# Three seven-product pairs per gate-up group, ring places for split weights and stored sums in an fp32 encoder layer

## The chip, the cores and the metric

The kernel runs on one core of a Trainium2 chip. The metric is device time in microseconds (us), the median of several executions. TensorE is called PE here (PEld is its weight load), VectorE DVE, ScalarE ACT, GpSimd POOL, and SP is the engine that issues most DMAs.

## What is computed

One encoder layer on x of 256 tokens by 2048 features, in fp32, weights drawn once per call from memory:

```
x = x + 0.5 * post1(swiglu_1(pre1(x)))
h = pre_m(x); p = h @ W_in
x = x + post_m(concat(hgrn2(p), attention(p)) @ W_out)
x = x + 0.5 * post2(swiglu_2(pre2(x)))

def swiglu(x, w_gate_up, w_down):
    gate, up = jnp.split(x @ w_gate_up, 2, axis=-1)
    return (jax.nn.silu(gate) * up) @ w_down
```

`w_gate_up` is 2048 x 11264 and `w_down` 5632 x 2048, so the two FFNs hold most of the work, and the change lies in them and in the helper that all stages use to split weights.

## The kernel before, in words

**Splits.** Every fp32 operand of a product is kept as two parts: an upper part h (ACT rounds it, L176) and a lower part l = value - h (DVE subtracts, L177; both lines are `split_act`). One block product is three matmuls into one PSUM bank, `three` (L417, issued at L423): upper by upper, upper by lower, lower by upper. Weights come by `load` (L141) as a `raw` tile of 128 x 2048 words, of which three places exist (`rawp`, L68). `split` (L158) cuts it by two calls of `split_half` (L168), 1024 columns each, into h and l places of 1024 columns; the pools `hip` and `lop` have five places each (L69, L70).

**Gate-up stage.** `Gated` (L793) does 11 groups of 512 gate and 512 up columns in each FFN. A group is eight pairs (u = 0 to 7), each pair a slice of 256 of the 2048 rows and so one raw tile of four blocks b11, b12, b21, b22 of 128 x 512. A plain pair (`plain`, L432) is eight block products, 24 matmuls. A pair that stands in `gated.sums` goes through `seven` (L445): seven products in place of eight (21 matmuls), of sums of weight blocks with sums of activation blocks. On the weight side `seven` splits b11 into a place of its own (`one_block`, L438, here a place of `hip` and `lop` of which half is used), adds on DVE at L455 (1024 columns), splits the lower half, adds at L459, splits the upper half, adds at L461 and splits the lower half again (`last`). Four extra banks p collect products that belong to several results; `fold` (L489) adds them to the four result banks c once per group, by one ACT copy (L495) and eight DVE adds (L496 to L503), issued just ahead of the products of the pair at position `after` + 1, where `after` is the position behind the last seven-product pair (L406). The two pairs around the fold have their products sorted by result bank. Which pairs are seven-product pairs is `MIXED_IN = (2, 4)` (L787). Their activation sums are made once per FFN by `even` (L860), during group 0; `begin` (L398) looks them up when a group begins, so group 0 of each FFN is all plain.

**Units.** Behind each group `units` (L881) makes silu(gate) * up (L886 ACT, L887 DVE), turns it by eight 128 x 128 transposes (L898) into two tiles `ht`, splits these, and for 11 of the 22 tiles (`MIXED`, L788) also makes four sums of 128 x 128 (`sums_of`, L378: L380, L383, L384). These are kept in fp32, in the room where X was and in other pools (`sums_room`, L850).

**Down stage.** `Pairs` (L540) multiplies the 22 tiles by `w_down` in two runs of 1024 result columns, 11 plain and 11 seven-product pairs in a run, in the order written out at L934. In each seven-product pair `left_sums` (L569) splits the fp32 sums of that tile into the tile `sp` again, in both runs, but for two tiles whose split is kept from run 0 to run 1 (`keep`). Here `seven` also loads and half splits the next plain pair from inside (`begin_next`, L505). The same class does the output projection of the middle stage (sums `sy`).

**Order.** The order of instructions on each engine is set when the kernel is built, from program order and the builder's own estimates of time; only the start (L959) and the end of each down stage (`finish`, L631) are issued as written. Every engine and DMA queue then works in its order.

Of the kernel before, what the change touches and what calls it, by code (L numbers as in the profile page):

```python
# [20 lines left out]
P = 128  # L21
# [16 lines left out]
def hymba_layer_kernel(  # L38
# [27 lines left out]
    const = ctx.enter_context(tc.tile_pool(name="const", bufs=1))  # L66
    xp = ctx.enter_context(tc.tile_pool(name="xp", bufs=1))
    rawp = ctx.enter_context(tc.tile_pool(name="rawp", bufs=3))  # L68
    hip = ctx.enter_context(tc.tile_pool(name="hip", bufs=5))  # L69
    lop = ctx.enter_context(tc.tile_pool(name="lop", bufs=5))  # L70
    psum = ctx.enter_context(tc.tile_pool(name="psum", bufs=4, space=bass.MemoryType.PSUM))
    dram = ctx.enter_context(tc.tile_pool(name="dram", bufs=1, space=bass.MemoryType.DRAM))

# [64 lines left out]
    scales = const.tile([P, 8], F32, tag="scales", name="scales")  # L138
    rs2, two, rest = (scales[:, 2 * i : 2 * i + 2] for i in range(3))

    def load(src, between=None):  # L141
        raw = rawp.tile([P, 2048], F32, tag="raw", name=nm("raw"))
        if len(src.shape) == 4:

            dst = raw.rearrange("p (a n b) -> p a n b", a=src.shape[1], n=src.shape[2])
            parts = [(dst[:, a], src[:, a]) for a in range(src.shape[1])]
        else:
            parts = [(raw.rearrange("p (a b) -> p a b", a=src.shape[1]), src)]
        for i, (to, of) in enumerate(parts):
            if i and between:  # L150
                between()
            nc.sync.dma_start(to, of)
        return raw

    def split_load(src, hp=hip, lp=lop, between=None, middle=None):
        return split(load(src, between), hp, lp, middle)

    def split(raw, hp=hip, lp=lop, middle=None):  # L158
        hs, ls = [], []
        for i in range(2):  # L160
            if i and middle:
                middle()
            h, l = split_half(raw, i, hp, lp)
            hs.append(h)
            ls.append(l)
        return hs, ls

    def split_half(raw, i, hp=hip, lp=lop):  # L168
        part = raw[:, i * 1024 : (i + 1) * 1024]
        h = hp.tile([P, 1024], F32R, tag="h", name=nm("h"))  # L170
        l = lp.tile([P, 1024], F32R, tag="l", name=nm("l"))
        split_act(h, l, part)
        return h, l

# [212 lines left out]
    class Blocks:  # L387
# [50 lines left out]
        def one_block(self):  # L438

            return (  # L440
                p.tile([P, 1024], F32R, tag=t, name=nm(t))[:, 0:512]
                for p, t in ((hip, "h"), (lop, "l"))
            )

        def seven(self, u, aside=None):  # L445

            raw = load(self.source(u))
            if aside:
                aside()
            b11, b12, b21, b22 = (raw[:, i * 512 : (i + 1) * 512] for i in range(4))  # L450
            four = raw.rearrange("p (i c) -> p i c", i=4)
            h, l = self.one_block()
            split_act(h, l, b11)

            nc.vector.tensor_tensor(  # L455
                four[:, 0:2], four[:, 0::3], four[:, 1:2].to_broadcast([P, 2, 512]), ALU.add
            )
            lower = split_half(raw, 1)
            nc.vector.tensor_tensor(b22, b11, b22, ALU.add)  # L459
            upper = split_half(raw, 0)  # L460
            nc.vector.tensor_tensor(b21, b22, b21, ALU.add)  # L461
            if aside:
                aside()
            last = split_half(raw, 1)
            if not self.p:
                self.p = [pa(), pa(), pb(), pb()]
            a, w = self.tiles[u], self.left_sums(u)

            def lhs(k, m):
                return [a[:, k, i, m * P : (m + 1) * P] for i in range(2)]  # L470

            def summed(j):
                return [w[:, j, i, :] for i in range(2)]

            def rhs(two, n):
                return [x[:, n * 512 : (n + 1) * 512] for x in two]

            for at, left, right in (
                (("p", 0), lhs(0, 0), (h, l)),
                (("c", 0, 0), lhs(1, 0), rhs(lower, 0)),  # L480
                (("c", 0, 1), summed(S4), rhs(lower, 1)),
                (("p", 1), summed(S1), rhs(upper, 0)),
                (("p", 3), summed(S3), rhs(upper, 1)),
                (("p", 2), summed(S2), rhs(last, 1)),
                (("c", 1, 0), lhs(1, 1), rhs(last, 0)),
            ):
                self.three(at, *left, *right)

        def fold(self):  # L489

# [49 lines left out]
    class Pairs(Blocks):  # L540
# [4 lines left out]
        HELD = 2  # L545
        AHEAD = True

        def __init__(self, w, orders, tiles, sums, room, gain_src, keep=()):

            super().__init__(tiles, sums)  # L550
            self.keep, self.kept = keep, {}
# [15 lines left out]
            return src.rearrange("(k p) c -> p k c", p=P)  # L567

        def left_sums(self, u):  # L569
            if u in self.kept:  # L570
                return self.kept[u]
            keep = self.now == 0 and u in self.keep
            tag = f"sp{u}" if keep else "sp"
            w = far["pool"].tile([P, 4, 2, P], F32R, tag=tag, name=nm("sp"), bufs=1 if keep else 2)
            split_act(w[:, :, 0, :], w[:, :, 1, :], self.sums[u])
            if keep:
                self.kept[u] = w
            return w

        def one_block(self):  # L580
            return (
# [49 lines left out]
        def finish(self, mul, post, new_x=None, gain=None, lead=None):  # L631
# [5 lines left out]
            self.work(n_order - self.HELD)  # L637
            held = []
            for u in order[n_order - self.HELD :]:
                held.append((u, *split_load(self.source(u), hp=post, lp=post)))  # L640
            close_far()
            self.half_gain(post)
            if new_x:
# [140 lines left out]
    NU = DFF // 256  # L784
    LATE = 8

    MIXED_IN = (2, 4)  # L787
    MIXED = (*range(0, 18, 2), 20, 21)  # L788

    def pair_of(xt, u):  # L790
# [2 lines left out]
    class Gated(Blocks):  # L793
# [13 lines left out]

        def left_sums(self, u):
            return self.sums[u]

        def see(self, xt):
            for u in range(KT // 2):
# [24 lines left out]
    def ffn(gated, w_dn, post_gain, again, gain=None, lead=None, aside=None):  # L837

        with ExitStack() as st:
# [5 lines left out]
            where_X_was = []  # L845

            def room_for(tag):
                return work.tile([P, 512], F32, tag=tag, name=nm(tag))

            def sums_room(u):  # L850
                n = MIXED.index(u)
                if n == 0:
                    where_X_was.append(xp.tile([P, 8, 4, P], F32, tag="X", name=nm("sums")))
                if n < 8:
                    return where_X_was[0][:, n]
                if n > 8:
                    return far["pool"].tile([P, 4, P], F32, tag=f"su{n}", name=nm("su"), bufs=1)
                return work.tile([P, 4, P], F32, tag=f"su{n}", name=nm("su"))

            def even(u):  # L860

                x = gated.tiles[u].rearrange("p k i t -> p (k i) t")
                nc.vector.tensor_tensor(
                    x, x.bitcast(F32), R[:, None, :].to_broadcast([P, 4, T]), ALU.mult
                )
                if u in MIXED_IN:
                    x = gated.tiles[u].bitcast(F32)
                    whole = room_for("z").rearrange("p (k t) -> p k t", k=2)
                    nc.vector.tensor_tensor(whole, x[:, :, 0, :], x[:, :, 1, :], ALU.add)
                    ws = sums_of(whole, room_for("s").rearrange("p (j t) -> p j t", j=4))  # L870
                    w = work.tile([P, 4, 2, P], F32R, tag="sp", name=nm("xs"), bufs=2)
                    split_act(w[:, :, 0, :], w[:, :, 1, :], ws)
                    gated.sums[u] = w

# [6 lines left out]
            def units(c, scale):  # L881
# [10 lines left out]
                for j in range(2):  # L892
# [15 lines left out]
                    split_act(ht[:, :, 0, :], ht[:, :, 1, :], u)  # L908
                    hts.append(ht)
                    if g in MIXED:  # L910
                        sums[g] = sums_of(u, sums_room(g))
                yield

            pre_stats()
# [1 line left out]
            for g in range(NG):  # L916
                if g:
                    gated.group(g)
                for u in range(gated.pos, KT // 2):
                    gated.work(u + 1)  # L920
                    if g == 0:
                        if u == 4:
                            power_and_rest()
                            spread(two)
                        for done in {4: (0, 1, 2), 5: (3, 4), 6: (5, 6), 7: (7,)}.get(u, ()):
                            even(done)
                        if u == 5 and aside:
                            aside()
                    if waiting and u == 0:
                        next(waiting)  # L930
                waiting = units(gated.c, rest if g else rs2)
                next(waiting)
            close_far()
            orders = [  # L934
                [1, 0, 3, 2, 4, 5, 6, 8, 7, 10, 9, 12, 11, 14, 13, 16, 15, 20, 21, 17, 18, 19],

                [1, 0, 2, 3, 4, 5, 6, 14, 7, 8, 9, 10, 16, 11, 12, 13, 20, 21, 15, 17, 18, 19],
            ]
            sums.update((u, None) for u in MIXED if u not in sums)
            rows = Pairs(w_dn, orders, hts, sums, work, post_gain, keep=(0, 2))  # L940
            rows.half_gain(far["pool"])
            rows.work(1)
            next(waiting)
# [15 lines left out]
    with tc.manual_schedule():  # L959
# [15 lines left out]
        h, l = (  # L975
            p.tile([P, 1024], F32R, tag=t, name=nm(t)) for p, t in ((hip, "h"), (lop, "l"))
        )

        def half(i):
            cs = slice(i * 512, (i + 1) * 512)  # L980
# [549 lines left out]
```

## Time and profile before

| | |
|---|---|
| median of 3 runs | 1864.88 us (1864.38 to 1866.83) |
| span of the profiled execution, first to last instruction | 1861.4 us |
| PE busy | 1840.7 us, 99% of the span |
| DVE busy | 1576.6 us, 85% |
| ACT busy | 1086.1 us, 58% |
| DMA | 365.78 MB, mean 197 GB/s |
| granted TensorE clock, mean | 0.998 of full speed (2.4 GHz level) |

The profiled execution has no time of its own beside its span; the runs' median lies 3.5 us above that span. The gate-up stages lie at about 10 to 487 us and 1150 to 1620 us, the down stages behind them to about 720 us and to the end. A matmul's record is longer than the step from one matmul to the next, since matmuls are pipelined; starts tell the pace.

### The profile page before, as it was taken

How to read it: one execution, taken by the hardware profiler on the slowest of the kernel's cores; microseconds unless marked ns; L12 is line 12 of the kernel's file. 1: busy time of each engine (PE TensorE's matmuls, PEld its weight loads, DVE VectorE, ACT ScalarE, POOL GpSimd, SP SyncE). 2: the span in 40 equal slices, each digit the busy share in tenths (PEclk: the TensorE clock that was granted, in tenths of full speed). 3: DMA queues.
4: the chain of work that ended last, by engine and by line, in shares of the span. 5: the costliest groups of instructions: out<-in, count | busy, mean ns of one | idle time of the engine just before them, and what ended most of it. 6: DMA issues, size and time to landing. Idle time of an engine off the chain costs nothing.

```text
span 1861.4 us, 23279 instructions
## 1 busy us (share of the span) xinstructions
PE 1840.7 (99%) x8658; PEld 1527.0 (82%) x8658; DVE 1576.6 (85%) x1988; ACT 1086.1 (58%) x1445; POOL 21.4 (1%) x39
## 2 busy tenths in 40 slices
PE   9999999999999999999999999999999999999997
PEld 6888888888878777888888887788888888878886
DVE  7978888888899998567787788888888788899997
ACT  6555555555566565676677655655555555566563
POOL 1000000000000000000000000000000000000000
PEclk9999999999999999999999999999999999999999
DMA  7555655555555465655565455565565556445564
GB/s 251 204 200 187 208 196 181 181 203 203 188 204 215 179 255 196 201 181 166 169 187 148 169 210 200 185 214 186 211 207 192 199 195 207 175 181 205 224 228 168
DMA packets 180880, 365.78 MB, mean 197 GB/s; under 512 B 9256, under 2 KB 56448, under 8 KB 180000
## 3 DMA queue, kind: packets, MB, share of 16 engines
q1 hardware_dynamic: 180416, 364.17, 56.2%
q8 instruction: 68, 1.11, 0.2%
q14 instruction: 44, 0.36, 0.1%
q0 software_dynamic: 352, 0.14, 0.0%
HBM read 360.06 MB, written 4.21 MB: 196 GB/s over the span
## 4 chain that ended last, share of the span: by engine, by line
PE 72%; DVE 17%; DMA 4%; ACT 3%; issue 3%; POOL 0%; SPq 0%; DVEq 0%; ACTq 0%; POOLq 0%
PE pa L423 28%; PE pb L423 26%; DVE l L177 9%; PE pa L299 8%; PE pa L304 4%; DMA raw<-in_w_ffn_down_dram 2%; DVE raw L455 2%; ACT h L176 2%; DVE raw L459 1%; DVE raw L461 1%; DVE la L177 1%; DMA raw<-in_w_ffn_gate_up_dram 1%; PE pa L354 1%; PE pa L352 1%; PE pa L353 1%
## 5 line engine op out<-in xcount | busy, mean ns | idle before, releaser
L176 ACT CAST h<-raw 128x1024 fp32r<-128x1024 f32 (+1 forms) x793 | 795.0, 1028 | 616.2 <-PE pb L423 316.7
L177 DVE TENSOR_TENSOR l<-raw,h 128x1024 fp32r<-128x1024 f32 (+1 forms) x793 | 925.9, 1192 | 202.3 <-ACT h L176 168.8
L423 PE MATMUL pa<-h,xt 128*128 128x512 f32 x1248 | 431.3, 392 | 0.0
L423 PE MATMUL pb<-h,xt 128*128 128x512 f32 x1168 | 407.3, 390 | 0.0
L423 PEld LDWEIGHTS pa<-h,xt 128*128 128x128 f32 x1248 | 234.1, 188 | 48.7 <-ACT h L176 0.8
L423 PEld LDWEIGHTS pb<-h,xt 128*128 128x128 f32 x1168 | 219.2, 188 | 46.0 <-DVE xt L232 0.5
L423 PE MATMUL pa<-l,xt 128*128 128x512 f32 x624 | 243.3, 390 | 0.1
L423 PE MATMUL pb<-l,xt 128*128 128x512 f32 x584 | 227.3, 389 | 0.0
L299 PE MATMUL pa<-xt,h 128*128 128x512 f32 x672 | 164.7, 394 | 0.0
L423 PE MATMUL pa<-h,ht 128*128 128x512 f32 x440 | 156.1, 390 | 0.4 <-ACT h L176 0.4
L423 PE MATMUL pb<-h,ht 128*128 128x512 f32 x440 | 155.0, 390 | 0.2
L299 PEld LDWEIGHTS pa<-xt,h 128*128 128x128 f32 x672 | 123.0, 188 | 23.6
L423 PEld LDWEIGHTS pa<-l,xt 128*128 128x128 f32 x624 | 117.2, 188 | 24.5 <-DVE l L177 1.1
L423 PEld LDWEIGHTS pb<-l,xt 128*128 128x128 f32 x584 | 109.7, 188 | 22.6
L455 DVE TENSOR_TENSOR raw<-raw 128x1024 f32<-128x1024 f32 x88 | 107.5, 1222 | 1.6
L423 PEld LDWEIGHTS pa<-h,ht 128*128 128x128 f32 x440 | 82.4, 188 | 18.7 <-ACT h L176 1.3
L423 PEld LDWEIGHTS pb<-h,ht 128*128 128x128 f32 x440 | 82.6, 188 | 17.9 <-DVE pb L501 1.0
L304 PE MATMUL pa<-xt,l 128*128 128x256 f32 x672 | 91.5, 285 | 0.0
L304 PEld LDWEIGHTS pa<-xt,l 128*128 128x128 f32 x672 | 87.1, 191 | 3.2
L423 PE MATMUL pa<-l,ht 128*128 128x512 f32 x220 | 86.2, 392 | 1.5 <-DVE l L177 1.5
L423 PE MATMUL pb<-l,ht 128*128 128x512 f32 x220 | 86.0, 391 | 0.1
L423 PE MATMUL pb<-h,sp 128*128 128x512 f32 x192 | 70.1, 395 | 2.3 <-ACT h L176 2.3
(281 smaller groups left out, 2179.4 us busy)
## 6 DMA issues: line engine op xcount, KB each, us to landing
raw<-in_w_ffn_gate_up_dram SPq DMA_DIRECT2D x350, 512.0 KB, 4.6
raw<-in_w_ffn_down_dram SPq DMA_DIRECT2D x88, 1024.0 KB, 5.4
raw<-in_w_mix_in_dram SPq DMA_DIRECT2D x52, 1024.0 KB, 5.0
raw<-in_w_mix_out_dram SPq DMA_DIRECT2D x16, 1024.0 KB, 5.0
pg<-in_post_norm_ffn_dram SPq DMA_DIRECT2D x4, 512.0 KB, 6.9
X<-in_x_dram SPq DMA_DIRECT2D x2, 1024.0 KB, 7.4
bias<-row SPq DMA_DIRECT2D x16, 128.0 KB, 4.6
kept<-X SPq DMA_DIRECT2D x2, 1024.0 KB, 4.9
```

Source lines behind the costliest of these rows:

```text
L176: nc.scalar.copy(hi, src)
L177: nc.vector.tensor_tensor(lo, src, hi.bitcast(F32), ALU.subtract)
L299: nc.tensor.matmul(slot[f], weights(hs, kk, f), xcol(xt, k), start=(k == 0), stop=(k == KT - 1))
L304: nc.tensor.matmul(slot[f][:, 0:T], weights(ls, kk, f), xcol(xt, kh * 8 + kk, 0), start=False, stop=False,)
L352: nc.tensor.matmul(dst, xh, h[:, o : o + n], start=(k == 0), stop=False)
L353: nc.tensor.matmul(dst, xh, l[:, o : o + n], start=False, stop=False)
L354: nc.tensor.matmul(dst, xl, h[:, o : o + n], start=False, stop=(k == KT - 1))
L423: nc.tensor.matmul(self.bank(at), lhs, rhs, start=(n == 1), stop=n in (ends, self.of[at]), skip_group_check=n > ends,)
L455: nc.vector.tensor_tensor(four[:, 0:2], four[:, 0::3], four[:, 1:2].to_broadcast([P, 2, 512]), ALU.add)
L459: nc.vector.tensor_tensor(b22, b11, b22, ALU.add)
L461: nc.vector.tensor_tensor(b21, b22, b21, ALU.add)
```

## The change

- `MIXED_IN` is (1, 3, 5): three of a gate-up group's eight pairs go by seven products, and the fold moves to the group's last pair. `one_block` of the gate-up stage no longer takes a ring place but alternates between two rooms where X was.
- The pools of h and l places become two tiles, `ring_h` and `ring_l`, of five places each, taken in turn by `places`. Where two places taken together lie side by side, one subtraction of 2048 columns makes both lower parts; where they run over the ring's end, there are two of 1024.
- `seven` splits `upper` and `last` together, behind both adds.
- The activation sums of the down stage are split once, when a unit is made, and stored to device memory by a DMA from POOL's queue (128 x 1024 words each); each seven-product pair of the down stage loads them by a DMA on SP's queue (`left_early`, four places). `keep` goes, and the order of the first run is another.

```diff
-    hip = ctx.enter_context(tc.tile_pool(name="hip", bufs=5))
-    lop = ctx.enter_context(tc.tile_pool(name="lop", bufs=5))
+    ringp = ctx.enter_context(tc.tile_pool(name="ringp", bufs=1))
...
+    RING = 5
+    ring_h, ring_l = (
+        ringp.tile([P, RING * 1024], F32R, tag=t, name=f"ring{t}") for t in "hl"
+    )
+    ring = [0]
+
+    def places(n):
+        out = []
+        while n:
+            at = ring[0] % RING
+            some = min(n, RING - at)
+            ring[0] += some
+            n -= some
+            cs = slice(at * 1024, (at + some) * 1024)
+            out.append((ring_h[:, cs], ring_l[:, cs]))
+        return out
...
+    def split(raw, pool=None):
+        if pool:
+            hs, ls = zip(*(split_half(raw, i, pool) for i in range(2)))
+            return hs, ls
         hs, ls = [], []
...
+        n = 0
+        for h, l in places(2):
+            some = h.shape[1]
+            part = raw[:, n : n + some]
+            n += some
+            for o in range(0, some, 1024):
+                nc.scalar.copy(h[:, o : o + 1024], part[:, o : o + 1024])
+                hs.append(h[:, o : o + 1024])
+                ls.append(l[:, o : o + 1024])
+            nc.vector.tensor_tensor(l, part, h.bitcast(F32), ALU.subtract)
         return hs, ls
...
         def seven(self, u, aside=None):
+            self.left_early(u)
             raw = load(self.source(u))
...
             lower = split_half(raw, 1)
             nc.vector.tensor_tensor(b22, b11, b22, ALU.add)
-            upper = split_half(raw, 0)
             nc.vector.tensor_tensor(b21, b22, b21, ALU.add)
             if aside:
                 aside()
-            last = split_half(raw, 1)
+            upper, last = zip(*split(raw))
...
         def left_sums(self, u):
-            if u in self.kept:
-                return self.kept[u]
-            keep = self.now == 0 and u in self.keep
...
+            if u in self.left:
+                return self.left.pop(u)
+            w = far["pool"].tile(
+                [P, 4, 2, P], F32R, tag="sp", name=nm("sp"), bufs=4 if self.stored else 2
+            )
+            if self.stored:
+                nc.sync.dma_start(w.bitcast(F32), self.sums[u])
+            else:
+                split_act(w[:, :, 0, :], w[:, :, 1, :], self.sums[u])
             return w
...
-    MIXED_IN = (2, 4)
+    MIXED_IN = (1, 3, 5)
...
+        def one_block(self):
+            self.blocks.reverse()
+            return self.blocks[0]
...
                     if g in MIXED:
-                        sums[g] = sums_of(u, sums_room(g))
+                        ws = sums_of(u, room_for("s").rearrange("p (j t) -> p j t", j=4))
+                        w = where_X_was(0).rearrange("p (j i t) -> p j i t", j=4, i=2)
+                        split_act(w[:, :, 0, :], w[:, :, 1, :], ws)
+                        sums[g] = dram.tile([P, 4, 2, P], F32, tag=f"ss{g}", name=nm("ss"))
+                        nc.gpsimd.dma_start(sums[g], w.bitcast(F32))
...
             orders = [
-                [1, 0, 3, 2, 4, 5, 6, 8, 7, 10, 9, 12, 11, 14, 13, 16, 15, 20, 21, 17, 18, 19],
+                [1, 3, 0, 5, 2, 4, 7, 6, 8, 9, 10, 11, 12, 13, 14, 15, 16, 20, 17, 21, 18, 19],
...
-            rows = Pairs(w_dn, orders, hts, sums, work, post_gain, keep=(0, 2))
+            rows = Pairs(w_dn, orders, hts, sums, work, post_gain, stored=True)
```

## Rows read from the trace of the kernel before

**Rows 1.** The page: busy time by engine, and the chain that ended last.
```profile
PE 1840.7 (99%) x8658; PEld 1527.0 (82%) x8658; DVE 1576.6 (85%) x1988; ACT 1086.1 (58%) x1445; POOL 21.4 (1%) x39
PE 72%; DVE 17%; DMA 4%; ACT 3%; issue 3%; POOL 0%; SPq 0%; DVEq 0%; ACTq 0%; POOLq 0%
```

**Rows 2.** Busy time of each engine in stretches; here one gate-up group's length.
```profile
core 0: us, PE busy (x) PEld busy (x) DVE busy (x) ACT busy (x) POOL busy (x), PEclk, DMA share, GB/s
273.00:316.00 43.00, 43.00 (x195) 35.72 (x194) 35.73 (x43) 22.94 (x27) 0.00 (x0) 1.00 0.56 196
```

**Rows 3.** The same view for stretches of the two down stages.
```profile
500.00:550.00 50.00, 48.93 (x209) 38.41 (x208) 49.10 (x59) 28.56 (x34) 0.00 (x0) 1.00 0.57 209
...
600.00:650.00 50.00, 49.36 (x216) 40.01 (x216) 46.94 (x52) 29.86 (x40) 0.00 (x0) 1.00 0.51 183
650.00:690.00 40.00, 40.00 (x176) 32.31 (x175) 38.77 (x44) 23.94 (x28) 0.00 (x0) 1.00 0.73 269
...
1630.00:1680.00 50.00, 49.23 (x212) 38.88 (x211) 49.96 (x62) 30.55 (x37) 0.00 (x0) 1.00 0.54 197
...
1730.00:1780.00 50.00, 50.00 (x221) 40.99 (x220) 47.82 (x52) 30.61 (x40) 0.00 (x0) 1.00 0.49 175
```

**Rows 4.** PE in order of time in one gate-up group: start us, us, what.
```profile
229.95 0.39 PE L423 MATMUL pb<-h,xt 128*128 128x512 f32 x1
...
235.39 0.39 PE L423 MATMUL pb<-h,xt 128*128 128x512 f32 x1
235.62 0.27 PE L898 MATMUL pa<-ident,z 128*128 128x128 f32 x1
...
236.41 0.48 PE L423 MATMUL pa<-h,xt 128*128 128x512 f32 x1
```

**Rows 5.** DVE in order of time: two groups' ends, both sevens of one group.
```profile
229.88 0.75 DVE L887 SCALAR_TENSOR_TENSOR z<-pa,scales,z 128x512 f32<-128x512 f32 x1
...
231.91 1.22 DVE L455 TENSOR_TENSOR raw<-raw 128x1024 f32<-128x1024 f32 x1
234.22 1.22 DVE L177 TENSOR_TENSOR l<-raw,h 128x1024 fp32r<-128x1024 f32 x1 [1.08 <-ACT h L176]
...
250.51 0.69 DVE L461 TENSOR_TENSOR raw<-raw 128x512 f32<-128x512 f32 x1
252.40 4.69 DVE L177 TENSOR_TENSOR l<-raw,h 128x1024 fp32r<-128x1024 f32 x4 [1.20 <-ACT h L176]
...
272.93 0.75 DVE L887 SCALAR_TENSOR_TENSOR z<-pa,scales,z 128x512 f32<-128x512 f32 x1
```

**Rows 6.** Groups by line and shape, whole span: count, busy us, mean ns, idle before.
```profile
L177 DVE TENSOR_TENSOR l<-raw,h 128x1024 fp32r<-128x1024 f32 x751 | 899.3, 1221 | 202.1 <-ACT h L176 168.7 <-PE pa L304 29.7
L176 ACT CAST h<-raw 128x1024 fp32r<-128x1024 f32 x751 | 769.3, 1051 | 614.9 <-PE pb L423 316.7 <-DVE raw L461 96.1 <-DVE raw L455 82.0
L177 DVE TENSOR_TENSOR sp<-sums,sp 128x512 fp32r<-128x512 f32 x28 | 19.2, 684 | 0.0
L177 DVE TENSOR_TENSOR sp<-su,sp 128x512 fp32r<-128x512 f32 x12 | 8.2, 685 | 0.0
```

**Rows 7.** Waits in two gate-up groups, 273 to 359 us: us in total, times, longest.
```profile
ACT h L176 <- PE pb L423: 30.3, 16, 3.9
DVE l L177 <- ACT h L176: 14.4, 13, 2.3
```

**Rows 8.** Waits in the first down stage, 500 to 690 us.
```profile
ACT ha L176 <- DMA raw<-in_w_ffn_down_dram: 9.2, 6, 2.3
DVE l L177 <- ACT h L176: 5.7, 9, 1.2
```

**Rows 9.** DMA issues: kind, engine, count, KB each, median us to landing.
```profile
raw<-in_w_ffn_down_dram SPq DMA_DIRECT2D x88, 1024.0 KB, 5.4
kept<-X SPq DMA_DIRECT2D x2, 1024.0 KB, 4.9
row<-bias_rows POOLq DMA_DIRECT2D x1, 16.0 KB, 1.8
```

More of the change, by code (lines that the diff above doesn't have):

```diff
@@ L153, in load, with split_load, split_half @@
         return raw
-    def split_load(src, hp=hip, lp=lop, between=None, middle=None):
-        return split(load(src, between), hp, lp, middle)
-    def split(raw, hp=hip, lp=lop, middle=None):
-        hs, ls = [], []
[L160 to L165, printed above, removed]
+    def split_load(src, pool=None, between=None):
+        return split(load(src, between), pool)
+    def split(raw, pool=None):
+        if pool:
+            hs, ls = zip(*(split_half(raw, i, pool) for i in range(2)))
+            return hs, ls
+        hs, ls = [], []
+        n = 0
[8 more added lines that the diff above has]
+            nc.vector.tensor_tensor(l, part, h.bitcast(F32), ALU.subtract)
         return hs, ls
-    def split_half(raw, i, hp=hip, lp=lop):
+    def split_half(raw, i, pool=None):
         part = raw[:, i * 1024 : (i + 1) * 1024]
-        h = hp.tile([P, 1024], F32R, tag="h", name=nm("h"))
-        l = lp.tile([P, 1024], F32R, tag="l", name=nm("l"))
+        if pool:
+            h, l = (pool.tile([P, 1024], F32R, tag=t, name=nm(t)) for t in "hl")
+        else:
+            [(h, l)] = places(1)
         split_act(h, l, part)
@@ L436, in plain @@
             self.three(("c", m, n), a[:, k, 0, ms], a[:, k, 1, ms], hs[k][:, cs], ls[k][:, cs])
[L438 to L443, printed above, removed]
         def seven(self, u, aside=None):
+            self.left_early(u)
             raw = load(self.source(u))
@@ L487, in seven, with left_early @@
                 self.three(at, *left, *right)
+        def left_early(self, u):
+            pass
         def fold(self):
@@ L546, in hymba_layer_kernel, with __init__ @@
         AHEAD = True
-        def __init__(self, w, orders, tiles, sums, room, gain_src, keep=()):
+        def __init__(self, w, orders, tiles, sums, room, gain_src, stored=False):
             super().__init__(tiles, sums)
-            self.keep, self.kept = keep, {}
+            self.stored, self.left = stored, {}
             self.w, self.orders = w, orders
@@ L569, in left_sums, with left_early @@
         def left_sums(self, u):
-            if u in self.kept:
-                return self.kept[u]
-            keep = self.now == 0 and u in self.keep
[L573 to L577, printed above, removed]
-            return w
+            if u in self.left:
[5 more added lines that the diff above has]
+                nc.sync.dma_start(w.bitcast(F32), self.sums[u])
+            else:
+                split_act(w[:, :, 0, :], w[:, :, 1, :], self.sums[u])
+            return w
+        def left_early(self, u):
+            if self.stored:
+                self.left[u] = self.left_sums(u)
         def one_block(self):
@@ L639, in finish @@
             for u in order[n_order - self.HELD :]:
-                held.append((u, *split_load(self.source(u), hp=post, lp=post)))
+                held.append((u, *split_load(self.source(u), post)))
             close_far()
@@ L844, in ffn, with where_X_was @@
             hts, sums = [], {}
-            where_X_was = []
+            rooms = []
             def room_for(tag):
                 return work.tile([P, 512], F32, tag=tag, name=nm(tag))
[L850 to L858, printed above, removed]
+            def where_X_was(i):
+                if not rooms:
+                    t = xp.tile([P, 4, 1024], F32R, tag="X", name=nm("rooms"))
+                    rooms.extend(t[:, i] for i in range(4))
+                return rooms[i]
             def even(u):
@@ L870, in even @@
                     ws = sums_of(whole, room_for("s").rearrange("p (j t) -> p j t", j=4))
-                    w = work.tile([P, 4, 2, P], F32R, tag="sp", name=nm("xs"), bufs=2)
+                    if MIXED_IN.index(u) == 2:
+                        w = where_X_was(1).rearrange("p (j i t) -> p j i t", j=4, i=2)
+                    else:
+                        w = work.tile([P, 4, 2, P], F32R, tag="sp", name=nm("xs"), bufs=2)
                     split_act(w[:, :, 0, :], w[:, :, 1, :], ws)
@@ L928, in ffn @@
                             aside()
+                        if u == 6:
+                            gated.blocks = [
+                                tuple(where_X_was(2 + i)[:, o : o + 512] for o in (0, 512))
+                                for i in range(2)
+                            ]
                     if waiting and u == 0:
@@ L973, in arrive @@
             nc.sync.dma_start(raw[:, i * 512 : (i + 1) * 512], first[:, i // 2, i % 2])
-        h, l = (
-            p.tile([P, 1024], F32R, tag=t, name=nm(t)) for p, t in ((hip, "h"), (lop, "l"))
-        )
+        [(h, l)] = places(1)
         def half(i):
```

## The prediction, made before the changed kernel ran

> **What bounds the kernel now.** I read the page first. PE is busy for 99% of the span and holds 72% of the chain that ended last, DVE 17% [rows 1]; so a matmul taken away counts, unless DVE, at 85%, has no room for what is put in its place. Both differ by stage, so the stretches come next.
>
> In the gate-up stage PE is never idle, and DVE is busy for 35.73 of 43.00 us [rows 2]. The cause of DVE's other 7 us shows in the waits: in two groups DVE stood 14.4 us until ACT's upper part came, while ACT stood 30.3 us for PE to free a place [rows 7]. The chain runs back to PE: DVE is ahead, and the five places are full. PE's order of time gives the pace: 24 steps from 229.95 to 235.39 us, 0.2267 us each, at the full granted clock; the eight transposes between units take 0.79 us [rows 4]. 186 matmuls and the transposes make 42.96 us; from one group's first L887 on DVE to the next it is 43.05 [rows 5]. Nothing is lost there.
>
> The down stage is otherwise. DVE is busy for 49.10 and 49.96 of 50 us in the first stretch of each [rows 3], and PE gets through 209, 216 and 212 matmuls where a full stretch has 221. These three lose 26 matmuls, 26 x 0.2267 = 5.9 us. There DVE is the bound, and it is filled to 98% and more in spite of the dependences inside `seven`: it stood only 5.7 us for ACT in 190 [rows 8].
>
> **The change, part by part.**
>
> Gate-up, PE. A third seven-product pair takes 24 - 21 = 3 matmuls from a group. Group 0 of each FFN has none, since the activation sums do not exist when it begins, so 2 x 10 groups change: 60 x 0.2267 = **-13.6 us**. By the record's length of 0.39 us [rows 4] it would be 23, but records overlap; starts decide. The group's bound by PE becomes 43.05 - 0.68 = 42.37 us.
>
> Gate-up, DVE. A plain pair that becomes a seven costs one 512 split, L455, L459, L461 and a third 1024 split more. Four 1024 splits back to back took 4.69 us and the last of them 1.22 alone, so a step is 1.16 [rows 5, 6]; a 512 step is by the same overlap 0.62, and L459 and L461, which wait for the one before, take 0.69 each. Sum: 0.62 + 2 x 1.16 + 1.38 = 4.32 us. The split of the down stage's sums, now made with the units, adds 0.62 per group (11 in 11 groups). The wide subtraction is in no row. From 684 ns for 512 columns to 1221 for 1024 [rows 6], 537 more per 512, I estimate 2.30 us for 2048, a step of 2.23, against two steps of 2.32 or two records of 2.44. It saves 0.09 to 0.15. Eight pairs of places are taken per group, and one in five runs over the ring's end: 6.4 x 0.09 = -0.5 us (-1.0 at most). DVE: 35.73 + 4.32 + 0.62 - 0.5 = **40.2 us** of 42.37, 95%. The nearest rows for such a load are the down stage's, 98% on DVE with PE still at 98% [rows 3]; so DVE holds the pace, but with 2.2 us per group to spare where it had 7.
>
> Three things eat of that. (a) The fold's eight adds move to the last pair, so one plain pair instead of two lies between it and the next seven, with the units' work. (b) `upper`'s split lay between the adds and `last`'s; now the wide subtraction waits for two ACT casts, the second of which starts only behind L461: 1.05 us plus issue, as the 1.20 us of idle in front of the split at 252.40 show [rows 5, 6]. Behind it on DVE stand the next pair's splits, and PE behind those. (c) A wide subtraction needs two places free at once, and occupies DVE for 2.3 us in which a fold add cannot pass. The cover is the other pair's work: the block splits of gate-up sevens no longer need a ring place. Bounds: 0 if all idle is covered; if both gaps of each seven (1.08 behind L455, 1.20 behind L461) stand open, 40.2 + 6.8 = 47.0 us a group. I take 0.15 us a group, near the covered end because the down stage fills DVE so well with the same dependences: **+3 us**.
>
> Down stage, DVE and PE. Forty splits of sums (28 + 12 in the rows) go, 20 per FFN at 0.62 = 12 us of a stage of some 225; sevens join two splits (22 per FFN, 2 us at most). DVE comes to about 92%. The ACT casts go as well. What PE can get back is the 5.9 us of the three stretches and a little between, 7 at most; the splits' wait for ACT behind L461 keeps some. **-4 us**, from -7 to 0.
>
> Down stage, DMA. 22 loads of 128 x 1024 words (0.52 MB) per FFN come onto SP's queue, each ahead of its raw tile's load. At the 269 GB/s that a dense stretch moved [rows 3] one takes 1.9 us. ACT waited 9.2 us in 190 for raw tiles already [rows 8], and behind ACT stand DVE's split and PE. Four places let the loads run far ahead and the DMA engines are at 51 to 74%, so most are hidden: **+1 us**, from 0 to 4 (44 x 1.9 = 84 if none were hidden, which the free share excludes).
>
> Stores. A unit's store has until the next group's unit, 42 us. Only tiles 20 and 21, made together in each FFN's last group, share the one room: 21's split on ACT and DVE waits for 20's store, with the down stage's first splits queued behind. A megabyte took 4.9 us on SP's queue [rows 9], half of one some 3 to 5; the ring's lead of two pairs, 10 us of PE, covers most. **+0.5 us each, +1**; below nothing is excluded, 8 at most.
>
> A rule of the Trainium skill speaks against this store: SBUF — State Buffer, in the box on the "DVE blocks DMA" trap, says that descriptors of a POOL-queue DMA are written by GpSimd, which DVE can lock out of the port they share, so that the DMA waits. The page names two-port modes for that, and fp32 subtractions are not among these; no run here shows a large store from POOL's queue. By it the sum gains the price of the third rival. The small one in the trace landed in 1.8 us with DVE at work [rows 9].
>
> Start and ends. At the kernel's start, issued as written, pair 1's lower part now waits for its second cast, and so does the first lead tile of the two `finish` chains that lead on: at most 1.05 + 1.1 us at each of three places, hidden where PE has queued products. **+1 us**, 0 to 4. One more set of sums in group 0's `even` (some 3 us of DVE, no seven-product pair in that group): 0; if its cover were gone, 3 per FFN. The middle stage only joins splits: 0.
>
> Sum: -13.6 + 3 - 4 + 1 + 1 + 1 = **-11.6 us**, on a span of 1861.4, so 1849.8. The runs' median lies 3.5 us above that span; I keep that: **1853.3 us**.
>
> **Rivals.**
>
> 1. *DVE becomes the bound of gate-up (slower).* Place: DVE behind L461, waiting for `last`'s cast, in three sevens per group. It decides once DVE's idle passes 2.2 us per group; beyond 43.05 - 40.2 = 2.85 the group is longer than before. For: 2.85 us is less than one wait of 1.2 per seven, 3.6; this stage does not load and cast the next pair from inside `seven`, as the down stage does. Against: the 98% of [rows 3]. With 3.6 us: 43.8 a group, 20 x 0.75 = +15, with the other terms (-1) +14: 1879 us. Chance 0.16.
> 2. *The gate-up gain is eaten (about no change).* Idle of about 2.5 us per group, for example from the fold's new place alone: 42.7 to 43, PE gains 0 to 7, the rest -1: 1857 to 1865. Chance 0.18, most of it within the bound.
> 3. *Stores starve (the skill's rule).* If 20's store took three times 4.9 us, ACT and DVE would stand 15 us, 5 to 10 beyond the ring's lead, in each FFN: +10 to +20, so 1863 to 1873. Chance 0.03.
> 4. *Loads of sums hold the raw tiles up.* Half of them exposed by 1 us: +22 in place of +1: 1874 us. Against: the DMA share. Chance 0.03.
>
> **How the numbers follow.** The forecast has 0.60. Measurement tells about 0.2% (3.7 us) from no change: faster is below 1861.1, slower above 1868.6. Faster: 0.60 and 0.06 of rival 2. Same: 0.11 of rival 2 and 0.04 of the borders of 1 and 3. Slower: the rest, 0.19. The forecast's own range is 1846 (all stalls of the down stage gone, none new) to 1861. The whole range reaches from 1845 to 1872, which leaves out the far half of rivals 1 and 4 and little below.
>
> **What would show it.** Right: groups of 42.4 to 42.6 us between L887 rows, DVE at 94 to 96% there with PE idle near 0; 2048-column subtractions of about 2.3 us; in the down stage 219 to 221 matmuls per 50 us and DVE near 92%. Wrong: groups above 43 us with PE waiting for DVE's l; an ACT cast in each FFN's last group standing several us for a DMA; or ACT waits on raw or sp loads that grow beyond 20 us per down stage.

## The result, and the profile after

The changed kernel took 1891.36 us (1887.27 to 1895.7, 4 runs) beside 1864.63 us before: a ratio of 1.0144, interval 1.0132 to 1.0156, so slower by 1.4%. I had forecast 1853.3 and a range up to 1872; the first rival had 1879. The profiled execution is the longest of the four (span 1893.9 us, +32.5 on before's).

The page of the changed kernel, busy time by engine and the chain that ended last, beside [rows 1]:

```profile
PE 1851.7 (98%) x8598; PEld 1511.1 (80%) x8598; DVE 1628.1 (86%) x1848; ACT 1110.9 (59%) x1473; POOL 32.4 (2%) x61
issue 51%; PE 33%; DVE 7%; DMA 5%; ACT 4%; POOL 1%; SPq 0%; DVEq 0%; POOLq 0%; ACTq 0%
```

The 60 matmuls are gone (8658 to 8598), yet PE's busy time rose. DVE has 140 instructions fewer and 51.5 us more to do.

Busy time in stretches of the changed kernel (span, then busy us and count for PE, PEld, DVE, ACT, POOL, then clock, DMA share, GB/s): groups 2 and 4 of the first FFN, the passage from group 0, the start of the first down stage, and the output projection.

```profile
112.00:155.00 43.00, 43.00 (x192) 34.68 (x191) 39.45 (x41) 24.76 (x29) 0.54 (x1) 1.00 0.61 208
198.00:242.00 44.00, 43.98 (x196) 35.07 (x195) 39.52 (x40) 24.60 (x30) 0.53 (x1) 1.00 0.59 203
...
45.00:70.00 25.00, 22.69 (x96) 16.81 (x95) 25.00 (x35) 11.67 (x15) 0.54 (x1) 1.00 0.42 138
...
501.00:551.00 50.00, 47.75 (x206) 38.51 (x205) 43.64 (x48) 25.89 (x31) 1.06 (x2) 0.97 0.84 307
...
1064.00:1158.00 94.00, 89.55 (x386) 72.26 (x385) 76.95 (x88) 51.53 (x69) 0.56 (x1) 0.98 0.56 202
```

DVE's load in a group is about what was worked out, 39.5 us where I had 40.2 and before's row had 35.73 [rows 2]. But from transposes to transposes groups 1 to 10 of the first FFN last 42.4 to 43.7 us and groups 2 to 10 of the second 42.6 to 44.3, instead of 42.4 to 42.6, while DVE is not full. In the passage from group 0 DVE has no idle time at all. At the down stage's start DVE is relieved (43.64 of 50, before 49.10 [rows 3]) and PE still gets through fewer matmuls, 206. The waits of the whole span name the link (us in total, times, longest):

```profile
PEld pa L449 <- DVE ringl L189: 38.8, 72, 2.8
...
PE pa L449 <- DVE ringl L189: 15.5, 20, 2.3
```

L189 is the joint subtraction. Before, all PE waits for a lower part in this view were below 6 us a row. Its form, and the 1024-column form that is left at L203:

```profile
L189 DVE TENSOR_TENSOR ringl<-raw,ringh 128x2048 fp32r<-128x2048 f32 x232 | 528.5, 2288 | 108.9 <-ACT ringh L186 93.4 <-PE pa L330 14.7
L203 DVE TENSOR_TENSOR ringl<-raw,ringh 128x1024 fp32r<-128x1024 f32 x177 | 215.0, 1220 | 13.4 <-ACT ringh L202 13.3
```

2288 ns is the estimate's 2.30 us. DVE stood 0.47 us in front of each (108.9 / 232), less than in front of the two 1024-column ones that it replaces (2 x 202.1 / 751 = 0.54 us, [rows 6]). So the price does not show in DVE's own time; it shows where PE waits.

**Where the time went.** A table of stage lengths, worked out from the starts of PE's instructions: group 0 to its units' transposes, groups 1 to 10 between the transposes behind groups 0 and 10, the down stage from there to the first turn of X, the middle stage to the first product of the output projection, that projection to the next turn of X, and the same for the second FFN, whose down stage is counted to the end of the last product. The kernels below before and after are the experiments.

```
                 group 0  1-10   down  middle  out   group 0' 1-10'  down'
before             63.4  430.6  227.3  331.6   86.9    57.0   430.2  225.5
after              69.8  431.4  230.1  333.0   94.1    63.7   434.0  229.6
e1_rings           65.9  430.3  229.6  332.6   96.8    60.4   428.8  227.0
e2_narrow          64.8  434.7  226.4  331.3   86.3    64.0   426.3  224.6
e3_pools           64.9  440.4  226.0  331.7   86.3    62.0   434.0  228.6
e4_two             65.7  431.1  229.3  333.0   95.5    58.6   431.6  229.3
e5_late            63.6  430.2  225.1  332.7   86.3    59.0   431.8  228.9
e6_widelate        67.5  429.0  233.4  332.6   91.3    64.8   430.7  231.1
e7_gatewide        68.1  431.2  223.6  331.7   86.3    63.7   431.6  230.8
e8_plainwide       69.8  433.2  225.6  332.6   86.3    63.8   434.3  227.8
e9_twonarrow       63.1  431.6  225.9  331.6   87.1    56.7   431.9  223.3
e10_joinednarrow   64.7  435.0  225.9  331.3   88.1    63.8   428.8  226.3
e11_room21         69.9  429.0  230.5  332.7   91.4    63.7   430.5  231.4
e12_best           63.2  430.1  225.6  332.6   86.3    59.0   431.0  225.8
```

From before to after: the two group 0s +6.4 and +6.7, the groups behind them +0.8 and +3.8, the down stages +2.8 and +4.1, the middle +1.4, the output projection +7.2, in all +33.2. The stage with no seven-product pair added and no store, the output projection, lost the most. What happens there, in order of time, on DVE, ACT and PE of the changed kernel:

```profile
1138.15 1.22 DVE L203 TENSOR_TENSOR l<-raw,h 128x1024 fp32r<-128x1024 f32 x1
1139.29 2.29 DVE L189 TENSOR_TENSOR ringl<-raw,ringh 128x2048 fp32r<-128x2048 f32 x1
...
1130.54 1.05 ACT L186 CAST ringh<-raw 128x1024 fp32r<-128x1024 f32 x1 [0.49 <-ACT y L517]
...
1137.97 1.06 ACT L186 CAST ringh<-raw 128x1024 fp32r<-128x1024 f32 x1 [0.32 <-PE pb L449]
...
1138.91 0.39 PE L449 MATMUL pb<-ringh,ya 128*128 128x512 f32 x1
1141.63 0.50 PE L449 MATMUL pa<-ringl,ya 128*128 128x512 f32 x1 [2.34 <-DVE ringl L189]
```

These are the casts and the subtraction of pair 7, a plain pair. Its first upper part was cast at 1130.54; its lower part could have followed. The second cast waited for PE to free the second place until 1137.97 (ACT cast for other pairs in between). The joint subtraction waited for both, ran to 1141.58, and PE, which needed the first 1024 columns only, stood 2.34 us. And a stall can have a second price, in the stretches around it:

```profile
1138.00:1142.00 4.00, 1.66 (x8) 1.07 (x7) 4.00 (x4) 1.03 (x1) 0.00 (x0) 1.00 0.27 59
1142.30:1145.30 3.00, 3.00 (x9) 2.35 (x8) 2.15 (x2) 1.59 (x2) 0.00 (x0) 0.50 1.03 386
```

PE was busy 1.66 of 4.00 us, and then its clock was granted at 0.50, the 1.2 GHz level: matmuls start 0.43 us apart (1142.99, 1143.42, 1143.85) in place of 0.2267. The changed kernel has three such stretches, behind stalls of 1.51, 2.19 and 2.34 us that end at 69, 524 and 1142 us; the kernel before has none but at its end.

### The profile page after: what moved, and what is told of

The parts are those of the page before. It is cut to its first block, busy times and chain, and to the rows that moved or that the text cites. A ratio compares the mean times of both kernels' runs of the same rounds, so it can differ in the third digit from the quotient of the medians.

```text
span 1893.9 us, 23018 instructions
## 1 busy us (share of the span) xinstructions
PE 1851.7 (98%) x8598; PEld 1511.1 (80%) x8598; DVE 1628.1 (86%) x1848; ACT 1110.9 (59%) x1473; POOL 32.4 (2%) x61
## 4 chain that ended last, share of the span: by engine, by line
issue 51%; PE 33%; DVE 7%; DMA 5%; ACT 4%; POOL 1%; SPq 0%; DVEq 0%; POOLq 0%; ACTq 0%
PE pa L449 8%; PE pa L325 8%; PE pb L449 8%; PE pa L330 4%; DVE ringl L189 3%; DMA raw<-in_w_ffn_down_dram 3%; DVE ringl L203 2%; ACT ringh L186 2%; DMA raw<-in_w_mix_out_dram 1%; PE pa L379 1%; PE pa L380 1%; PE pa L378 1%; ACT ringh L202 1%; DMA ss<-rooms 1%; POOL ss L945 1%
## 5 line engine op out<-in xcount | busy, mean ns | idle before, releaser
L186 ACT CAST ringh<-raw 128x1024 fp32r<-128x1024 f32 x582 | 600.8, 1051 | 364.9 <-PE pb L449 144.3
L189 DVE TENSOR_TENSOR ringl<-raw,ringh 128x2048 fp32r<-128x2048 f32 (+1 forms) x350 | 668.9, 1928 | 121.1 <-ACT ringh L186 98.3
L449 PE MATMUL pa<-ringh,xt 128*128 128x512 f32 x1048 | 368.0, 391 | 1.8 <-DVE pa L522 1.7
L449 PE MATMUL pb<-ringh,xt 128*128 128x512 f32 x1048 | 365.8, 392 | 2.3 <-ACT ringh L186 1.5
L449 PEld LDWEIGHTS pb<-ringh,xt 128*128 128x128 f32 x1048 | 196.8, 188 | 48.2 <-ACT ringh L186 2.9
L449 PEld LDWEIGHTS pa<-ringh,xt 128*128 128x128 f32 x1048 | 196.7, 188 | 44.1 <-DVE pa L522 2.9
L202 ACT CAST ringh<-raw 128x1024 fp32r<-128x1024 f32 (+1 forms) x179 | 186.7, 1046 | 73.0 <-PE pb L449 39.4
L203 DVE TENSOR_TENSOR ringl<-raw,ringh 128x1024 fp32r<-128x1024 f32 (+1 forms) x179 | 216.3, 1214 | 13.5 <-ACT ringh L202 13.5
L449 PE MATMUL pa<-ringl,xt 128*128 128x512 f32 x524 | 206.5, 394 | 5.8 <-DVE ringl L189 4.0
L449 PE MATMUL pb<-ringl,xt 128*128 128x512 f32 x524 | 204.5, 390 | 0.0
```

The costliest lines, as they stand in the source:

```text
L186: nc.scalar.copy(h[:, o : o + 1024], part[:, o : o + 1024])
L189: nc.vector.tensor_tensor(l, part, h.bitcast(F32), ALU.subtract)
L202: nc.scalar.copy(hi, src)
L203: nc.vector.tensor_tensor(lo, src, hi.bitcast(F32), ALU.subtract)
L449: nc.tensor.matmul(self.bank(at), lhs, rhs, start=(n == 1), stop=n in (ends, self.of[at]), skip_group_check=n > ends,)
```

## The experiments

Two theories first. **W**: the wide subtraction costs in every stage. **S**: the third seven makes DVE the bound of gate-up. The runs compare with the kernel before on the same chip (1865.40, 1863.94 and 1864.84 us in the three sets).

**e1_rings.** Of the change only the rings, the joint subtractions and the joined split:

```diff
+    ring_h, ring_l = (ringp.tile([P, RING * 1024], F32R, ...) for t in "hl")
-            upper = split_half(raw, 0)
...
-            last = split_half(raw, 1)
+            upper, last = zip(*split(raw))
```

> The kernel before with the rings, the 2048-column subtractions and the joined split of upper and last; two seven-product pairs per group and the sums as before. Theory W (the wide subtraction, which waits for two casts and two free places, costs in every stage): 1880 to 1888 us, +15 to +23, with PE stalls at the start, in group 0, in the output projection and the down stages. Theory S (the third seven-product pair makes DVE the bound of gate-up): 1862 to 1868, about no change.

1878.93 us, 1.0073 (1.0055 to 1.009): a little below W's band, far above S's. The groups behind group 1 stay at 43.1 us; start, down stages and above all the output projection (96.8) lose.

**e2_narrow.** The changed kernel, narrow again, upper's split in its old place:

```diff
-            nc.vector.tensor_tensor(l, part, h.bitcast(F32), ALU.subtract)
+                nc.vector.tensor_tensor(ls[-1], part[:, o : o + 1024], hs[-1].bitcast(F32), ALU.subtract)
...
+            upper = split_half(raw, 0)
...
-            upper, last = zip(*split(raw))
+            last = split_half(raw, 1)
```

> The changed kernel with the rings, but every lower part by a subtraction of 1024 columns and upper's split between the two adds again. Theory W: 1855 to 1868 us, groups of 42.4 to 42.8 us. Theory S: 1889 to 1896 us, groups of 43.2 us and more, since DVE has a little more to do.

1871.39 us, 1.0032 (1.0021 to 1.0043): 20 us below the changed kernel, but above W's band. Output projection and down stages are below before. In steady groups it does what the prediction said; groups 4 and 5:

```profile
200.00:243.00 43.00, 42.84 (x195) 35.24 (x194) 40.01 (x49) 25.26 (x30) 0.53 (x1) 1.00 0.61 208
243.00:286.00 43.00, 42.98 (x196) 35.31 (x194) 39.76 (x48) 25.41 (x30) 0.53 (x1) 1.00 0.61 208
...
65.00:113.00 48.00, 45.02 (x190) 34.85 (x190) 44.43 (x53) 25.64 (x31) 0.59 (x1) 0.96 0.57 195
```

DVE at 39.8 to 40.0 us a group (the forecast's 40.2 without the 0.5 for the wide form is 40.7), groups of 42.4 to 42.9 us behind group 2 of the first FFN. What is lost lies in the third line: group 1 takes 48.1 us and group 2 44.5. So W is right for 20 us, and S's cost is there too, but in the passage, not in the steady state.

**e3_pools.** As e2_narrow, with `hip` and `lop` in place of the rings:

```diff
-    ringp = ctx.enter_context(tc.tile_pool(name="ringp", bufs=1))
+    hip = ctx.enter_context(tc.tile_pool(name="hip", bufs=5))
+    lop = ctx.enter_context(tc.tile_pool(name="lop", bufs=5))
```

> As e2_narrow, with pools of five places instead of the rings, so that a place is taken where one is free. Theory W: 1850 to 1866 us; below e2_narrow by as much as the fixed turn of the ring costs by itself. Theory S: 1889 to 1896 us.

1886.06 us, 1.0118 (1.0097 to 1.0138). Both theories miss, S by 3 us only. The rings do not cost: against pools they gain 15 us with three sevens. The passage lasts longer with pools, groups 1 to 4 at 47.5, 44.7, 43.9 and 46.3 us.

**e4_two.** The changed kernel with `MIXED_IN = (2, 4)`.

```diff
-    MIXED_IN = (1, 3, 5)
+    MIXED_IN = (2, 4)
```

> The changed kernel with MIXED_IN = (2, 4): rings, wide subtractions, stored sums, but two seven-product pairs per group and the fold in its old place. Theory W: 1885 to 1895 us, groups at 43.05 us, the stalls of start, output projection and down stages still there. Theory S: 1860 to 1868 us.

1884.50 us, 1.0105 (1.009 to 1.012), just below W's band and far above S's. With the wide subtraction the third seven costs 6.9 us (1891.36 - 1884.50).

Theory **G** then: without the wide subtraction steady groups hold the forecast, and the rest lies in group 0 and the passage.

**e5_late.** e2_narrow with pair 1's sums made in group 1:

```diff
-                if u in MIXED_IN:
+                if u in MIXED_IN[1:]:
+                    sums_in(u)
...
+                    if g == 1 and u == 2:
+                        sums_in(MIXED_IN[0])
```

> e2_narrow with the activation sums of pair 1 made in group 1 rather than in group 0, so that group 1 has two seven-product pairs and groups 2 to 10 have three. Theory G (without the wide subtraction, steady groups hold 42.4 to 42.9 us as predicted, and what is lost lies in group 0 and in the passage to group 1, where DVE is full): 1856 to 1861 us, groups 0 and 1 as in the kernel before, below it by 4 to 9 us. Theory S (the third seven costs everywhere): 1868 to 1872.

1865.51 us, 1.0001 (0.999 to 1.0012): between G and S. Group 0 and group 1 are back (63.6 and 43.4 us), but group 2, now the first with three, takes 44.3, and in the second FFN some steady groups take 44 to 45. (The profiled execution is the longest of the ten, which reach from 1858.43 to 1867.62 us.)

**e6_widelate.** The same edit on the changed kernel.

> The changed kernel as it is, rings and 2048-column subtractions, with the same delay of pair 1's sums to group 1. Theory G: 1879 to 1885 us, less by the 4 to 5 us that each group 0 costs, the losses of output projection and down stages unchanged. If the wide subtraction itself overfills group 0: 1888 to 1892.

1885.10 us, 1.0107 (1.009 to 1.0124): 6 us less than the changed kernel, just above what G said; group 0 of the second FFN did not gain in the profiled execution (64.8).

**e7_gatewide.** Joint subtractions in the gate-up groups only:

```diff
+    class Gated(Blocks):
+        WIDE = True
...
-            upper, last = zip(*split(raw))
+            if self.WIDE:
+                upper, last = zip(*split(raw, wide=True))
+            else:
+                last = split_half(raw, 1)
```

> The changed kernel with 2048-column subtractions in the gate-up groups only; start, middle stage, output projection, down stages and lead tiles subtract 1024 columns at a time, with upper's split between the adds. Theory W: 1870 to 1877 us, the output projection back at 87 us and each down stage at 225 to 227. If the wide subtraction costs mostly in gate-up: 1885 and more.

1877.48 us, 1.0072 (1.0053 to 1.009), at W's edge: of the 20 us between the changed kernel and e2_narrow, 13.9 (1891.36 - 1877.48) go with the wide form and the joint split outside gate-up and 6.1 with those inside. The output projection is back at 86.3 and the first down stage at 223.6; the second, expected at 225 to 227, takes 230.8 with no wide subtraction in it. So the second down stage does not tell the width's cost: with upper and last subtracted apart or by 1024 columns it takes 223.3 to 230.8 us in these runs, with the joint form in all stages 227.0 to 231.4. The first does: 223.6 to 227.3, and 229.3 to 233.4.

**e8_plainwide.** Joint subtractions for plain pairs, upper and last apart in `seven`:

```diff
+            upper = split_half(raw, 0)
             nc.vector.tensor_tensor(b21, b22, b21, ALU.add)
-            upper, last = zip(*split(raw))
+            last = split_half(raw, 1)
```

> The changed kernel with 2048-column subtractions for plain pairs and the middle stage, but in seven upper's and last's splits apart, upper's between the adds. If joining upper and last is what costs (its cover behind L461 is gone): 1870 to 1876 us. If the wide subtraction itself costs, two places and two casts to wait for: 1884 to 1892.

1881.03 us, 1.0092 (1.0077 to 1.0107), between the two. In the output projection and the first down stage the loss is gone, so there `seven`'s joint split is needed for it, though the stall shown above is a plain pair's. Pair 7 still has its joint subtraction in this run:

```profile
1125.34 1.05 ACT L186 CAST ringh<-raw 128x1024 fp32r<-128x1024 f32 x1 [0.32 <-PE pb L449]
...
1126.64 2.28 DVE L189 TENSOR_TENSOR ringl<-raw,ringh 128x2048 fp32r<-128x2048 f32 x1
```

It is done at 1128.92, and PE does not wait for it. By the code, the joint split puts `upper`'s place in the ring behind that of pair 6's first half. In the changed kernel pair 7's second place is then the one of that half, which PE reads up to its last products (1137.94); with `upper` split first it is `upper`'s own, free when the seven products are done. So in the output projection the loss comes from the two together. In gate-up (69.8, 433.2, 434.3) the plain pairs' joint subtraction costs as much by itself.

**e9_twonarrow.** e2_narrow with `MIXED_IN = (2, 4)`.

> e2_narrow with MIXED_IN = (2, 4): rings, 1024-column subtractions, stored sums, two seven-product pairs. It leaves only the rings' fixed turn, the stored sums and the down stage's order beside the kernel before. If these three are sound (as the stage lengths of e2_narrow say): 1861 to 1865 us, groups at 43.05, down stages 225 to 227 us, output projection 86 to 87. If the fixed turn or the stores cost by themselves: 1868 and more.

1860.15 us (1856.99 to 1863.47, 10 runs), 0.9976 (0.9967 to 0.9985): slightly below what was expected, and the one version that beats the kernel before, by 0.24%. Its groups take 43.1 us; the down stages, 225.9 and 223.3, give 1.4 and 2.2 us back.

**e10_joinednarrow.** Upper and last split together, but by 1024 columns (only e2_narrow's first edit).

> The changed kernel with every lower part by 1024 columns, but upper and last still split together behind both adds. If the place of upper's split is what the output projection and the down stages lose by: output projection 92 us and more, down stages 229 us and more, 1880 to 1888. If it is the width (the second cast and the second place): 86 to 88 and 225 to 227, 1868 to 1876.

1873.84 us, 1.0047 (1.0031 to 1.0062): place alone costs 2.4 us more than e2_narrow, which the intervals do not tell apart. It is the width that costs: output projection 88.1 against 94.1, and 17.5 us in all.

**e11_room21.** The changed kernel with a room of its own for tile 21's sums:

```diff
-                        w = where_X_was(0).rearrange("p (j i t) -> p j i t", j=4, i=2)
+                        w = where_X_was(int(g == MIXED[-1])).rearrange(
+                            "p (j i t) -> p j i t", j=4, i=2
+                        )
```

The wait that it removes, on ACT in the changed kernel:

```profile
515.97 0.62 ACT L202 CAST rooms<-s 128x512 fp32r<-128x512 f32 x1 [5.17 <-DMA ss<-rooms]
```

> The changed kernel, but tile 21's sums are split into a room of their own, so that their cast does not wait for tile 20's store. If that wait of 5.2 us on ACT makes the stall at each down stage's start: 1884 to 1888 us, down stages shorter by 2 to 4 us each, the wait gone from ACT's rows. If the ring's lead covers it and the stall has another cause: 1889 to 1893.

1892.44 us, 1.0147 (1.0133 to 1.0161): nothing gained, though the wait is gone, and with it, in the profiled execution, all half-clock stretches but the one at the end. The down stages still take 230.5 and 231.4; with the cast earlier PE waits elsewhere. That theory fell.

**e12_best.** e5_late with e11's room.

> e5_late with tile 21's sums in a room of their own: rings, 1024-column subtractions, three seven-product pairs from group 2 on, stored sums. If what is left in e5_late are the down stages' starts and single stalls: 1857 to 1863 us, 0.1 to 0.4% below the kernel before. If DVE, at 93% in these groups, keeps passing every delay on to PE: 1863 to 1867, no change that can be told.

1864.63 us, 1.0 (0.9991 to 1.0009): no change that can be told, the second expectation.

## Why the prediction was wrong

Steps in medians: kernel before 1864.8, rings, rooms for the block splits, stores and order (e9) -4.7, third seven (e2) +11.2, joined split (e10) +2.4, width +17.5, which makes 1891.4. The runs come from different sets, whose befores differ by 1.5 us, and the steps hold in this order only: with two sevens, joined split and width cost 24.4 us together (e4_two - e9_twonarrow), with three 20.0.

By stages, the sum had -13.6 + 3 for groups 1 to 10, which measured +4.6; 0 for group 0, but for the start's part of +1, which measured +13.1; -4 + 1 + 1 for the down stages, which measured +6.9; and 0 for the middle stage with the output projection, which measured +8.6.

- **The wide subtraction was put down as a saving.** The step that failed is "It saves 0.09 to 0.15", -0.5 us a group, with the waits under (b) and (c) taken as covered at +3 us, the middle stage at 0 and start and ends at +1. It measured +17.5 us with three sevens. As the output projection shows, its price is not in its duration: the first half's lower part, which PE wants first, waits for the second half's cast and place. PE's four waits of 0.50 to 2.34 us there come to 4.4 us of the 7.2 lost, and the half-clock stretch adds some 1.4 (7 steps of 0.43 in place of 0.2267 us). I named both waits, but priced them only in gate-up and weighed them against the down stage's 98% [rows 3], which had been reached with narrow splits that start as soon as one place is free. That row was no bound for the wide form.
- **Group 0 was costed at 0.** The third seven (e2_narrow - e9_twonarrow) cost 11.2 us where the sum had -13.6 + 3. "No seven-product pair in that group" overlooked that DVE also has to prepare group 1's first pairs there, with pair 1 now a seven. (e5_late, which takes both pair 1's sums and its seven out of this passage, brings groups 0 and 1 nearly back; how the loss divides between the two is not shown.) Before, this stretch already had no room:

```profile
45.00:70.00 25.00, 25.00 (x114) 19.82 (x113) 24.07 (x35) 10.71 (x14) 0.55 (x1) 1.00 0.49 169
```

  24.07 of 25 us on DVE, a stretch for which the prediction had no row. The bound that I gave, 3 us per FFN, was too small too: in e2_narrow group 0 to group 2 take 7.9 and 5.5 us longer than before (157.4 - 149.5 at group 2's transposes; 148.3 - 142.8, counted from the end of the output projection, in the second FFN).
- **The steady gate-up groups were right, without the wide form.** DVE's load measured 39.8 to 40.0 us (40.7 by the sum, without the wide form's -0.5), and groups of 42.4 to 42.9 us bear out the -0.68 less some stalls. But that is 0.3 us a group in effect, some 5 us in 16 groups, less than the passage costs. As built, with the wide form, groups 3 to 10 took 345.8 and 350.0 us against 344.4.
- **The first rival had the sign, and a small part of the place.** In the changed kernel's groups DVE is idle for some 3.5 us of 43, beyond the rival's 2.85, and groups 1 to 10 are longer than before, but by 0.8 and 3.8 us in place of 15. DVE is not full there; PE waits for a single late instruction, longest for a cast (1.63 us at 1452) and for adds of the fold (0.88 us at 1604, 0.68 at 406), which (a) had named. Most of the loss lies outside these groups.
- **The down stages' terms, -4 + 1 + 1, sum to -2 for both;** without the wide form e9_twonarrow measured -1.4 and -2.2, -3.6 together. With the loads, the start moves 316 GB/s and has fewer matmuls than later; PE's waits of that stretch are put down to DVE (1.6 us in three), so a price of the loads is not shown:

```profile
495.00:545.00 50.00, 48.40 (x213) 38.92 (x212) 45.95 (x54) 28.97 (x35) 1.06 (x2) 1.00 0.83 316
545.00:595.00 50.00, 50.00 (x223) 41.40 (x222) 46.56 (x49) 29.89 (x32) 0.00 (x0) 1.00 0.74 274
```

  In the changed kernel it turned to +2.8 and +4.1. For the first of these e10_joinednarrow (225.9 against 230.1) and the other runs without the wide form (at most 227.3) speak for the width; the second lies within what that stage also takes without it (up to 230.8). The fourth rival's sign came in part: ACT's waits for raw tiles, 20 and 21 us per down stage before, are 20 and 35 in the changed kernel. But in e10_joinednarrow they are 28 and 29, with stages of 225.9 and 226.3, so they do not set the length.
- **The stores** held 21's cast for 5.17 us, just above my 3 to 5, and cost nothing that e11_room21 could find, where the sum had +1. The third rival fell: the stores landed in 3.0 to 6.9 us, median 4.9, with DVE at 92% in the groups. The Trainium skill (SBUF — State Buffer, the box on the "DVE blocks DMA" trap) names two-port modes only, and the trace agrees: DVE's fp32 subtractions starved no store.

Left open: how much of the width's cost is the wait itself and how much the other order that the builder then chose for the engines; and which of rings, rooms, stores and order gives e9's 4.7 us. The single steady groups of 44 to 45 us that e5_late and e12_best have in the second FFN each hold one stall of PE of 1.36 to 1.69 us. In all four the trace puts it down to DVE's `ht` at L205, which reads a transposed unit out of a `pb` bank:

```profile
1375.35 0.47 PE L451 MATMUL pb<-ringh,xs 128*128 128x512 f32 x1 [1.68 <-DVE ht L205]
```

Pair 1 as a seven, right behind the transposes, takes four banks more; that it waits here for the one that `ht` still holds is likely by the code, but no run tests it. Why only some groups have the stall stays open.

## What to carry to other kernels

Joining two instructions saves one fixed cost and makes the first half's reader wait for the second half's inputs; where the reader stands right behind, price that wait with the place that comes free last, in every stage that shares the helper. An engine's mean load over a steady stretch says whether a change fits there; the passages into it, where work of two stages meets, need their own row. A removed product is worth its pace only where the engine that feeds it keeps its lead.

## What was not expected

- A five-place ring taken in fixed turn beat pools of five places by 15 us (e2_narrow against e3_pools); why is not shown.
- Stalls of 1.51 to 2.34 us on PE were followed by about 3 us at the 1.2 GHz level, three times in the changed kernel and never in e9_twonarrow before its end, so that a stall's price can be more than its length. It need not be: in e11_room21 the output projection has a stall of 2.24 us, and the granted clock stays at 1.00 behind it.
- The kernel before repeats within 1862.75 to 1868.32 us over 21 runs; e5_late, with DVE at 93% in its groups, spread from 1858.43 to 1867.62 over 10. That little slack makes the runs scatter is not shown: e12_best, as loaded (39.7 to 39.9 of 43 us), stayed within 1862.89 to 1867.33 over 11.
